# Batched x·yᵀ on one core: 24 unrolled groups rewritten as a loop of 4 iterations over 6 groups, with staggered semaphore resets and the loads of an iteration at its head

## The chip, the cores and the metric

One core of a Trainium2 chip. The metric is the device time of one execution in microseconds (us). Each experiment was timed in rounds with the kernel before on the same chip. A ratio is the mean time of one kernel's fast runs over that of the other's in the same rounds, so it is not quite the ratio of the medians quoted beside it.

Engines: PE is TensorE, DVE is VectorE, ACT is ScalarE, POOL is GpSimd, SP is the sync engine, which issues all transfers here. "L52" is line 52 of the kernel profiled.

## The reference

```python
def setup_inputs():
    batch, n_heads, seq_t, seq_s, channels = 8, 12, 512, 512, 64
    ...  # x, y: (8, 12, 512, 64) float32

def reference(x, y):
    return np.einsum('bhtc,bhsc->bhts', x, y).astype(np.float32)
```

The inputs are 25.2 MB together, the output 100.7 MB. Each byte is moved once.

## The kernel before

The 96 heads are taken in 24 groups of four. A group loads y and x (512 KB each), casts them to bf16 on POOL, transposes them on PE, multiplies on PE, copies the products from PSUM to SBUF on ACT and DVE, and stores 4 MB. Everything is unrolled in Python, so every address is a constant.

```python
    xv = x.rearrange("b h t c -> (b h t c)").rearrange("(g p n) -> g p n", p=P, n=R * C)
    ...  # yv and ov alike
    lpool = ctx.enter_context(tc.tile_pool(name="lpool", bufs=6))
    ...  # bpool 2, tpool 2, opool 4 buffers; PSUM: ptpsum 2, pmpsum 3

    def load(g):
        xs = lpool.tile([P, R * C], fp32)
        ys = lpool.tile([P, R * C], fp32)
        nc.sync.dma_start(ys, yv[g])
        nc.sync.dma_start(xs, xv[g])
        loaded[g] = (xs, ys)

    for g in range(6):
        load(g)

    def prepare(g, made):
        xs, ys = loaded.pop(g)
        ...  # cast y and x to bf16 on POOL
        if g + 6 < NG:
            load(g + 6)                      # prefetch, as soon as the buffers are cast
        yield
        ...  # transposes on PE, copies to SBUF on DVE and ACT, in three steps

    for g in range(NG):
        ...
        steps = prepare(g + 1, made) if g + 1 < NG else iter(())
        ot = opool.tile([P, R, S], fp32)
        edge = g == 0 or g == NG - 1
        for k in range(K):
            ...  # 8 matmuls into pm; copy pm to ot on ACT (even k) or DVE (odd k)
            if edge and k % 2 == 1:
                nc.sync.dma_start(ov[g][:, a:b], ...)          # four pieces of 1 MB
        if not edge:
            nc.sync.dma_start(ov[g], ot.rearrange("p r s -> p (r s)"))   # 4 MB
```

Of the kernel before, what the change touches and what calls it, by code (L numbers as in the profile page):

```python
# [1 line left out]

# [5 lines left out]


@with_exitstack  # L10
def kernel(
    ctx: ExitStack,
    tc: tile.TileContext,
    x: bass.AP,
    y: bass.AP,
    out: bass.AP,
):



    nc = tc.nc
    B, H, T, C = x.shape
    _, _, S, _ = y.shape
    P = 128
    G = 4
    Q = P // G
    R = T // Q
    NG = B * H // G
    K = R // 2
    fp32 = mybir.dt.float32  # L30
    bf16 = mybir.dt.bfloat16
    assert C * 2 == P and S == T and R == 16

    xv = x.rearrange("b h t c -> (b h t c)").rearrange("(g p n) -> g p n", p=P, n=R * C)
    yv = y.rearrange("b h t c -> (b h t c)").rearrange("(g p n) -> g p n", p=P, n=R * C)
    ov = out.rearrange("b h t s -> (b h t s)").rearrange("(g p n) -> g p n", p=P, n=R * S)

    const = ctx.enter_context(tc.tile_pool(name="const", bufs=1))
    lpool = ctx.enter_context(tc.tile_pool(name="lpool", bufs=6))
    bpool = ctx.enter_context(tc.tile_pool(name="bpool", bufs=2))  # L40
    tpool = ctx.enter_context(tc.tile_pool(name="tpool", bufs=2))
    opool = ctx.enter_context(tc.tile_pool(name="opool", bufs=4))
    ptpool = ctx.enter_context(tc.tile_pool(name="ptpsum", bufs=2, space=bass.MemoryType.PSUM))
    pmpool = ctx.enter_context(tc.tile_pool(name="pmpsum", bufs=3, space=bass.MemoryType.PSUM))

    loaded = {}

    def load(g):
        xs = lpool.tile([P, R * C], fp32)
        ys = lpool.tile([P, R * C], fp32)  # L50
        nc.sync.dma_start(ys, yv[g])
        nc.sync.dma_start(xs, xv[g])  # L52
        loaded[g] = (xs, ys)

    for g in range(6):
        load(g)

    ident = const.tile([P, P], bf16)
    make_identity(nc, ident)

    def prepare(g, made):

        xs, ys = loaded.pop(g)
        yb = bpool.tile([P, R, 2, C], bf16)
        nc.gpsimd.tensor_copy(  # L65
            yb, ys.rearrange("p (r c) -> p r c", c=C).unsqueeze(2).to_broadcast([P, R, 2, C])
        )
        xb = bpool.tile([P, R * C], bf16)
        nc.gpsimd.tensor_copy(xb, xs)  # L69
        if g + 6 < NG:  # L70
            load(g + 6)
        yield
        yT = tpool.tile([P, G * Q, R], bf16)
        xT = tpool.tile([P, K, P], bf16)
        for half in range(2):
            pt = ptpool.tile([P, K, P], bf16)
            for k in range(K):
                nc.tensor.transpose(  # L78
                    pt[:, k, :], yb[:, half * K + k].rearrange("p a c -> p (a c)"), ident
                )  # L80
            dst = yT[:, :, half * K:(half + 1) * K]
            src = pt.rearrange("p k n -> p n k")
            if half == 0:
                nc.vector.tensor_copy(dst, src)  # L84
            else:
                nc.scalar.activation(dst, src, mybir.ActivationFunctionType.Copy)  # L86
            yield
        pt = ptpool.tile([P, K, P], bf16)
        for k in range(K):
            nc.tensor.transpose(pt[:, k, :], xb[:, k * P:(k + 1) * P], ident)  # L90
        nc.vector.tensor_copy(xT, pt)  # L91
        made[g] = (xT, yT.rearrange("p n k -> p (n k)"))
        yield

    made = {}
    for _ in prepare(0, made):
        pass
    for g in range(NG):
        xT, yT = made.pop(g)
        steps = prepare(g + 1, made) if g + 1 < NG else iter(())  # L100
        ot = opool.tile([P, R, S], fp32)
        edge = g == 0 or g == NG - 1
        for k in range(K):
            if k % 2 == 0:
                next(steps, None)
            pm = pmpool.tile([P, 2, S], fp32)
            for h in range(G):
                for par in range(2):
                    nc.tensor.matmul(  # L109
                        pm[h * Q:(h + 1) * Q, par, :],  # L110
                        xT[par * C:(par + 1) * C, k, h * Q:(h + 1) * Q],
                        yT[par * C:(par + 1) * C, h * S:(h + 1) * S],
                        start=True, stop=True,
                    )
            if k % 2 == 0:
                nc.scalar.activation(ot[:, 2 * k:2 * k + 2, :], pm, mybir.ActivationFunctionType.Copy)  # L116
            else:
                nc.vector.tensor_copy(ot[:, 2 * k:2 * k + 2, :], pm)  # L118
            if edge and k % 2 == 1:
                a, b = (2 * k - 2) * S, (2 * k + 2) * S  # L120
                nc.sync.dma_start(ov[g][:, a:b], ot.rearrange("p r s -> p (r s)")[:, a:b])
        if not edge:
            nc.sync.dma_start(ov[g], ot.rearrange("p r s -> p (r s)"))  # L123


# [1 line left out]
_INS = ['x', 'y']  # L127
_OUTS = [((8, 12, 512, 512), 'float32')]


# [23 lines left out]
```

## Time and profile before

| | before |
|---|---|
| time | 309.24 us, median of 2 runs (309.17 to 309.3) |
| DMA | 126 MB, mean 410 GB/s, q1 takes 96.7% of 16 engines' span |
| PE, DVE, ACT busy | 51%, 51%, 39% |
| instruction fetches (q8) | 16 |
| issue of a 4 MB store to its landing | 36.6 us |

From the page: the span, the busy share of the DMA engines in 40 slices (tenths, 9 is 90% or more) with the rate in GB/s, the queues, the chain of waits that ended last, and the issues with their median time to landing.

```profile
span 307.5 us, 4865 instructions
...
DMA  7999999999999999999999999999999999999970
GB/s 288 417 376 425 449 405 462 412 427 435 415 436 429 404 450 420 432 436 409 448 426 404 457 420 413 451 412 443 428 431 431 437 431 420 439 432 426 410 302 21
...
q1 hardware_dynamic: 11232, 125.83, 96.7%
q8 instruction: 16, 0.26, 0.3%
...
DMA 72%; DVE 11%; PE 2%; issue 1%; ACT 1%; POOL 1%; SPq 0%; DVEq 0%; ACTq 0%
...
out_dram<-ot SPq DMA_DIRECT2D x22, 4096.0 KB, 36.6
ys<-in_y_dram SPq DMA_DIRECT2D x24, 512.0 KB, 35.7
```

The DMA row is full from the second slice to the last but two: the kernel is bound by transfers.

The waits of SP in the same kernel (in order: who waited, for what, us in total, how often, longest) show what it is held by. L123 is the store, L51 and L52 are the loads:

```profile
SPq L52 <- DMA out_dram<-ot: 130.1, 15, 9.9
SPq L123 <- DVE ot L118: 76.5, 21, 12.3
```

In this trace a store waits for the copy that makes its data (now and then for a load). Loads wait for a landed store because at most eight transfers are out at once: the trace never has more than eight issued and not landed (the compiled program has eight lanes on which landings are reported; the ninth load of the trace is issued at 4.54 us, after the first has landed at 4.08).

### The profile page before, as it was taken

The numbers are of one execution on the slowest core, as the hardware profiler recorded it, in microseconds if no ns is written. First come the engines' busy times: TensorE is split into PE (matmuls) and PEld (weight loads), VectorE is DVE, ScalarE is ACT, GpSimd is POOL, SyncE is SP. The second block draws the span as 40 slices with busy tenths as digits, with TensorE's granted clock in tenths as the row PEclk, the third lists the DMA queues.
The fourth block names the chain that finished last, engine by engine and source line by source line (L and its number), as shares of the span: only waits on it lengthen the run. The fifth ranks groups of instructions, "written<-read, shape, count | busy, mean of one in ns | idle before, by whom it ended". The sixth has DMA issues, their size and how long they took to land.

```text
span 307.5 us, 4865 instructions
## 1 busy us (share of the span) xinstructions
PE 158.3 (51%) x2112; PEld 81.2 (26%) x2112; DVE 157.3 (51%) x144; ACT 119.1 (39%) x121; POOL 70.6 (23%) x54
## 2 busy tenths in 40 slices
PE   2877775483564735648447474383754854320000
PEld 2443342341322313224133241231413412000000
DVE  0599997275373643736537356373563775340000
ACT  1587856144162341623506336053261564330000
POOL 5863354132122221222212312132121000000000
PEclk9999998556655667575575755757555575555555
DMA  7999999999999999999999999999999999999970
GB/s 288 417 376 425 449 405 462 412 427 435 415 436 429 404 450 420 432 436 409 448 426 404 457 420 413 451 412 443 428 431 431 437 431 420 439 432 426 410 302 21
DMA packets 11253, 126.14 MB, mean 410 GB/s; under 512 B 1248, under 2 KB 1248, under 8 KB 7392
## 3 DMA queue, kind: packets, MB, share of 16 engines
q1 hardware_dynamic: 11232, 125.83, 96.7%
q8 instruction: 16, 0.26, 0.3%
q14 instruction: 5, 0.04, 0.0%
HBM read 25.17 MB, written 100.66 MB: 409 GB/s over the span
## 4 chain that ended last, share of the span: by engine, by line
DMA 72%; DVE 11%; PE 2%; issue 1%; ACT 1%; POOL 1%; SPq 0%; DVEq 0%; ACTq 0%
DMA out_dram<-ot 71%; DVE ot L118 8%; DVE yT L84 2%; PE pm L109 1%; DMA ys<-in_y_dram 1%; ACT ot L116 1%; DVE xT L91 1%; PE pt L78 1%; POOL yb L65 1%; PE pt L90 0%; ACT yT L86 0%; SPq L123 0%; DVEq L118 0%; ACTq L116 0%
## 5 line engine op out<-in xcount | busy, mean ns | idle before, releaser
L118 DVE COPY ot<-pm 128x1024 f32<-128x1024 f32 x96 | 114.8, 1221 | 91.0 <-DMA out_dram<-ot 77.2
L116 ACT ACTIVATE ot<-pm 128x1024 f32<-128x1024 f32 x96 | 96.0, 1023 | 143.9 <-DMA out_dram<-ot 121.2
L109 PE MATMUL pm<-yT,xT 64*32 64x512 bf16 x1536 | 98.0, 555 | 100.6 <-ACT ot L116 84.0
L109 PEld LDWEIGHTS <-xT 64*32 64x32 bf16 x1536 | 30.0, 96 | 156.2 <-issue 142.9
L65 POOL CAST yb<-ys 128x2048 bf16<-128x2048 f32 x24 | 45.5, 1896 | 96.9 <-DMA ys<-in_y_dram 79.6
L78 PE MATMUL pt<-ident,yb 128*128 128x128 bf16 x384 | 42.8, 278 | 7.2 <-POOL yb L65 6.1
L69 POOL CAST xb<-xs 128x1024 bf16<-128x1024 f32 x24 | 25.0, 1042 | 65.1 <-PE pt L90 65.1
L78 PEld LDWEIGHTS <-yb 128*128 128x128 bf16 x384 | 35.5, 131 | 15.5 <-issue 7.8
L84 DVE COPY yT<-pt 128x1024 bf16<-128x1024 bf16 x24 | 29.2, 1215 | 7.2 <-PE pt L78 7.2
L90 PE MATMUL pt<-ident,xb 128*128 128x128 bf16 x192 | 26.4, 284 | 5.6 <-ACT yT L86 4.9
L86 ACT ACTIVATE yT<-pt 128x1024 bf16<-128x1024 bf16 x24 | 24.5, 1019 | 8.6 <-PE pt L78 8.6
L91 DVE COPY xT<-pt 128x1024 bf16<-128x1024 bf16 x24 | 16.6, 690 | 17.5 <-PE pt L90 17.5
L90 PEld LDWEIGHTS <-xb 128*128 128x128 bf16 x192 | 16.9, 127 | 18.1 <-issue 18.1
L86 ACT ACT_TABLE_LOAD x1 | 1.3, 1283 | 0.7 <-PEq L138 0.7
masks.py:199 POOL TENSOR_SCALAR_AFFINE_SELECT ident<-ident 128x128 bf16<-128x128 bf16 x1 | 0.3, 294 | 0.1
masks.py:197 POOL MEMSET ident<- 128x128 bf16 x1 | 0.2, 205 | 0.3 <-POOLq L138 0.3
L138 POOL MEMSET const-float32-0.0<- 128x1 f32 x1 | 0.1, 99 | 0.2 <-issue 0.2
L138 POOL MEMSET const-bfloat16-1.0<- 128x1 bf16 x1 | 0.1, 102 | 0.0
L138 POOL MEMSET const-uint8-127<- 128x1 uint8 x1 | 0.1, 102 | 0.0
L138 POOL MEMSET const-float32-1.0<- 128x1 f32 x1 | 0.1, 99 | 0.0
## 6 DMA issues: line engine op xcount, KB each, us to landing
out_dram<-ot SPq DMA_DIRECT2D x22, 4096.0 KB, 36.6
ys<-in_y_dram SPq DMA_DIRECT2D x24, 512.0 KB, 35.7
xs<-in_x_dram SPq DMA_DIRECT2D x24, 512.0 KB, 27.3
out_dram<-ot SPq DMA_DIRECT2D x8, 1024.0 KB, 23.6
```

The costliest lines, as they stand in the source:

```text
L65: nc.gpsimd.tensor_copy(yb, ys.rearrange("p (r c) -> p r c", c=C).unsqueeze(2).to_broadcast([P, R, 2, C]))
L69: nc.gpsimd.tensor_copy(xb, xs)
L78: nc.tensor.transpose(pt[:, k, :], yb[:, half * K + k].rearrange("p a c -> p (a c)"), ident)
L84: nc.vector.tensor_copy(dst, src)
L86: nc.scalar.activation(dst, src, mybir.ActivationFunctionType.Copy)
L90: nc.tensor.transpose(pt[:, k, :], xb[:, k * P:(k + 1) * P], ident)
L91: nc.vector.tensor_copy(xT, pt)
L109: nc.tensor.matmul(pm[h * Q:(h + 1) * Q, par, :], xT[par * C:(par + 1) * C, k, h * Q:(h + 1) * Q], yT[par * C:(par + 1) * C, h * S:(h + 1) ...
L116: nc.scalar.activation(ot[:, 2 * k:2 * k + 2, :], pm, mybir.ActivationFunctionType.Copy)
L118: nc.vector.tensor_copy(ot[:, 2 * k:2 * k + 2, :], pm)
L138: nc = _bacc.Bacc("TRN2", target_bir_lowering=False, num_devices=1)
```

## The change

The intent is less code: one body of six groups, which the engines run four times, instead of 24 copies. With the staggered mode, the body is cut into four stages and semaphores are reset stage by stage instead of behind a barrier. The loads of an iteration come at its head. The addresses are now a register (the loop's variable) plus a constant. The core of the diff:

```diff
+    BODY = 6
-    ov = out.rearrange("b h t s -> (b h t s)").rearrange("(g p n) -> g p n", p=P, n=R * S)
+    ov = out.rearrange("b h t s -> (b h t s)").rearrange("(r n) -> r n", n=R * S)
     ... (xv, yv alike)
-        nc.sync.dma_start(ys, yv[g])
-        nc.sync.dma_start(xs, xv[g])
+        nc.sync.dma_start(ys, yv[bass.ds(g, P)])
+        nc.sync.dma_start(xs, xv[bass.ds(g, P)])
     ...
-        if g + 6 < NG:
-            load(g + 6)
     ...
-    for g in range(NG):
+    with tc.For_i(0, NG * P, BODY * P, iteration_sync="staggered") as g0:
+        loaded = [load(g0 + i * P) for i in range(BODY)]
     ... (prepare the first group, then)
+        for i in range(BODY):
     ...
-        edge = g == 0 or g == NG - 1
+            edge = i == 0
     ...
-        if not edge:
-            nc.sync.dma_start(ov[g], ot.rearrange("p r s -> p (r s)"))
+            if not edge:
+                nc.sync.dma_start(ov[bass.ds(g0 + i * P, P)], ot.rearrange("p r s -> p (r s)"))
```

More of the change, by code (lines that the diff above doesn't have):

```diff
@@ L32 @@
     assert C * 2 == P and S == T and R == 16
-    xv = x.rearrange("b h t c -> (b h t c)").rearrange("(g p n) -> g p n", p=P, n=R * C)
-    yv = y.rearrange("b h t c -> (b h t c)").rearrange("(g p n) -> g p n", p=P, n=R * C)
-    ov = out.rearrange("b h t s -> (b h t s)").rearrange("(g p n) -> g p n", p=P, n=R * S)
+    xv = x.rearrange("b h t c -> (b h t c)").rearrange("(r n) -> r n", n=R * C)
+    yv = y.rearrange("b h t c -> (b h t c)").rearrange("(r n) -> r n", n=R * C)
+    ov = out.rearrange("b h t s -> (b h t s)").rearrange("(r n) -> r n", n=R * S)
     const = ctx.enter_context(tc.tile_pool(name="const", bufs=1))
@@ L44 @@
     pmpool = ctx.enter_context(tc.tile_pool(name="pmpsum", bufs=3, space=bass.MemoryType.PSUM))
-    loaded = {}
+    ident = const.tile([P, P], bf16)
+    make_identity(nc, ident)
     def load(g):
@@ L50, in load, with prepare @@
         ys = lpool.tile([P, R * C], fp32)
-        nc.sync.dma_start(ys, yv[g])
-        nc.sync.dma_start(xs, xv[g])
-        loaded[g] = (xs, ys)
-    for g in range(6):
-        load(g)
-    ident = const.tile([P, P], bf16)
-    make_identity(nc, ident)
-    def prepare(g, made):
-        xs, ys = loaded.pop(g)
+        nc.sync.dma_start(ys, yv[bass.ds(g, P)])
+        nc.sync.dma_start(xs, xv[bass.ds(g, P)])
+        return xs, ys
+    def prepare(xs, ys, made):
         yb = bpool.tile([P, R, 2, C], bf16)
@@ L91, in prepare @@
         nc.vector.tensor_copy(xT, pt)
-        made[g] = (xT, yT.rearrange("p n k -> p (n k)"))
+        made.append((xT, yT.rearrange("p n k -> p (n k)")))
         yield
-    made = {}
-    for _ in prepare(0, made):
-        pass
-    for g in range(NG):
-        xT, yT = made.pop(g)
-        steps = prepare(g + 1, made) if g + 1 < NG else iter(())
-        ot = opool.tile([P, R, S], fp32)
-        edge = g == 0 or g == NG - 1
-        for k in range(K):
-            if k % 2 == 0:
-                next(steps, None)
-            pm = pmpool.tile([P, 2, S], fp32)
-            for h in range(G):
-                for par in range(2):
-                    nc.tensor.matmul(
-                        pm[h * Q:(h + 1) * Q, par, :],
-                        xT[par * C:(par + 1) * C, k, h * Q:(h + 1) * Q],
-                        yT[par * C:(par + 1) * C, h * S:(h + 1) * S],
-                        start=True, stop=True,
-                    )
-            if k % 2 == 0:
-                nc.scalar.activation(ot[:, 2 * k:2 * k + 2, :], pm, mybir.ActivationFunctionType.Copy)
-            else:
-                nc.vector.tensor_copy(ot[:, 2 * k:2 * k + 2, :], pm)
-            if edge and k % 2 == 1:
-                a, b = (2 * k - 2) * S, (2 * k + 2) * S
-                nc.sync.dma_start(ov[g][:, a:b], ot.rearrange("p r s -> p (r s)")[:, a:b])
-        if not edge:
-            nc.sync.dma_start(ov[g], ot.rearrange("p r s -> p (r s)"))
@@ new lines @@
+    with tc.For_i(0, NG * P, BODY * P, iteration_sync="staggered") as g0:
+        loaded = [load(g0 + i * P) for i in range(BODY)]
+        made = []
+        for _ in prepare(*loaded[0], made):
+            pass
+        for i in range(BODY):
+            xT, yT = made[i]
+            steps = prepare(*loaded[i + 1], made) if i + 1 < BODY else iter(())
+            ot = opool.tile([P, R, S], fp32)
+            edge = i == 0
+            for k in range(K):
+                if k % 2 == 0:
+                    next(steps, None)
+                pm = pmpool.tile([P, 2, S], fp32)
+                for h in range(G):
+                    for par in range(2):
+                        nc.tensor.matmul(
+                            pm[h * Q:(h + 1) * Q, par, :],
+                            xT[par * C:(par + 1) * C, k, h * Q:(h + 1) * Q],
+                            yT[par * C:(par + 1) * C, h * S:(h + 1) * S],
+                            start=True, stop=True,
+                        )
+                if k % 2 == 0:
+                    nc.scalar.activation(ot[:, 2 * k:2 * k + 2, :], pm, mybir.ActivationFunctionType.Copy)
+                else:
+                    nc.vector.tensor_copy(ot[:, 2 * k:2 * k + 2, :], pm)
+                if edge and k % 2 == 1:
+                    a, b = (2 * k - 2) * S, (2 * k + 2) * S
+                    nc.sync.dma_start(
+                        ov[bass.ds(g0 + i * P, P), a:b],
+                        ot.rearrange("p r s -> p (r s)")[:, a:b],
+                    )
+            if not edge:
+                nc.sync.dma_start(ov[bass.ds(g0 + i * P, P)], ot.rearrange("p r s -> p (r s)"))
```

## The prediction

> **What bounds it now.** The DMA engines. The page gives DMA 97% of 16 engines' span, 126 MB at 410 GB/s; PE and DVE are busy 51%. The chain of waits is 71% store landings. Compute has slack: unstalled (timeline, 18 to 43 us) a group takes 6.25 us; at a granted clock of 0.5 about 7.5 us (an estimate: eight matmuls took 0.6 us, a transpose 0.11). In the steady part a group's traffic takes 12.65 us: two loads of 1.24 us and a store of 10.15 us, by the steps between landings.
>
> One DMA engine is the limit: from 300 to 306 us the windows read a DMA share of 0.06, one engine of 16. The landing records show its lag behind the next engine growing by about 0.4 us per group until 277 us, then standing at 6.5 us. The 16 instruction fetches of 16 KB (queue q8, about 0.95 us each) run from 18 to 258 us, so I take the lag to be these: at this engine's 26 GB/s each costs 0.63 us, 10 us in all. That all ride on one engine is inferred.
>
> **What the change does.**
> - Traffic and arithmetic stay: 12.65 x 6 = 76 us of DMA per iteration.
> - Prefetch across groups goes: 12 loads at an iteration's head (14.9 us), queued behind the last iteration's stores, then six stores. At the start of before, the first store was issued 10.8 us after ys had landed; with 1.3 us for that landing, 12.1 us, inside the 14.9 us of loads. Group 1's store follows 10 us later (24.9 against 14.9 us), as group 0's pieces take 10.1 us. So the queue hardly empties: 0 to 1 us in all.
> - Stage waits: I expect each quarter of the body to wait until the stores of the quarter two before have landed. Compute per iteration is some 6 x 7 + 12 us plus four refills of 2 to 3 us, about 65 us of 76. The next loads should be issued with two groups of stores still queued, some 14 us ahead. Hidden.
> - Code: PE's body is about 1056 instructions plus waits[...]. [...] No trace here shows a loop yet. If PE keeps its body, fetches fall to about 5 and time falls by up to 6.4 us (the next engine's lag).
> - Start and end: register set-up and the loop's exit, +1 us (a guess).
>
> **Sum.** 309.2 + 3 (fetches) + 1 (ends) + 0 to 1 (bubbles) = **313.5 us**, 8 in 10 within 308 to 321. Chances: faster by over 2% 0.04, within 2% 0.66, slower 0.30.
>
> **What would show it.** DMA share at 0.9 or more in nearly all slices; at most shallow dips at about 79, 155 and 231 us. q8 packets 20 to 24. ACT, DVE and PE idle some 14 us at each boundary, ended by the ys DMA. Chain still DMA above 65%. A single DMA engine at the end.
>
> **What would make it wrong.** Stage waits that hold SP or an engine until the store queue is empty: the DMA row would show holes below 0.7, and the time would be 325 or more. Slow DMA issue from register addresses (over 1.2 us each against 0.33 to 0.45 now) would starve the head. Fewer fetches: 303 to 308.

The 3 us for fetches was the author's estimate: 4 to 8 fetches more than the 16 of before, at 0.63 us each (16 KB at the 26 GB/s that the windows of before read from 300 to 306 us). Of these, the number of fetches was not shown; the 20 to 24 packets further down rest on it too. Estimates, without a trace, are also the "about 5" fetches and the four refills of 2 to 3 us (before has no stages to show one).

## The result, and the profile after

The kernel after takes 375.5 us (374.78 and 376.22) against 309.24: a ratio of 1.214, with 95% interval 1.204 to 1.224. The prediction was 313.5 us, 308 to 321.

The lines of the page after that answer to those shown of before:

```profile
span 373.0 us, 5474 instructions
...
DMA  6956877999986688797987759887999766998877
GB/s 201 409 203 286 365 341 337 394 394 394 343 332 231 275 358 373 337 390 341 450 324 294 281 225 394 383 348 337 394 394 368 278 268 267 394 394 373 358 337 337
...
q1 hardware_dynamic: 12096, 125.83, 82.1%
q8 instruction: 3, 0.05, 0.0%
...
DMA 66%; issue 17%; SPq 4%; DVE 1%; PE 1%; ACT 0%; ACTq 0%
...
out_dram<-ot SPq DMA_DIRECT2D x20, 4096.0 KB, 11.1
out_dram<-ot SPq DMA_DIRECT2D x16, 1024.0 KB, 4.0
ys<-in_y_dram SPq DMA_DIRECT2D x24, 512.0 KB, 11.3
```

The DMA row has holes nearly everywhere, not only at the three boundaries. The chain is still mostly DMA, so that share tells nothing here. What tells is the time to landing: 11.1 us in place of 36.6. Each 4 MB store now meets an empty queue. The waits of SP name the reason (L121 is the whole store, L116 the 1 MB piece):

```profile
SPq L121 <- DMA out_dram<-ot: 171.9, 16, 11.0
SPq L116 <- DMA out_dram<-ot: 40.2, 12, 5.5
```

SP no longer waits for the copy but for the landing of another store: 28 times, 212 us. In the chain of waits, in order of time (start, us, what), the second iteration reads:

```profile
112.93 5.96 DMA out_dram<-ot
...
119.06 3.99 DMA out_dram<-ot
...
123.07 3.83 DMA out_dram<-ot
...
131.67 11.37 DMA out_dram<-ot
...
143.19 11.13 DMA out_dram<-ot
...
154.45 11.09 DMA out_dram<-ot
...
165.67 11.09 DMA out_dram<-ot
```

Each store is issued only when the one before it has landed. The compiled program shows the wait: the waits of SP's stores, in order of issue, by the lanes on which transfers report their landing (a number and the stage; the first piece and the last two stores of the body are left out):

```
31 L116 DMACopy out_0_dram<-ot_153 128x2048 [waits DMAHW1_I-81_stg1, ...]
33 L116 DMACopy out_0_dram<-ot_153 128x2048 [waits DMAHW2_I-81_stg1]
35 L116 DMACopy out_0_dram<-ot_153 128x2048 [waits DMAHW0_I-81_stg2]
37 L121 DMACopy out_0_dram<-ot_274 128x8192 [waits DMAHW1_I-81_stg2]
39 L121 DMACopy out_0_dram<-ot_392 128x8192 [waits DMAHW0_49, ...]
41 L121 DMACopy out_0_dram<-ot_510 128x8192 [waits DMAHW1_49, ...]
```

Each waits for the lane of the store just before it. In the packet records of the trace, no DMA engine at all moves anything for 54.6 us in all, in 37 gaps, most of 1.2 to 1.5 us. Before had none once its first load was under way. An iteration takes 92.2 us (first load issued at 85.98, 178.19 and 270.40 us) instead of some 76.

My first theory: with register addresses, the framework's dependency tracking cannot tell the stores' targets in the output apart, takes them to overlap, and orders them by waits. Rivals: the staggered stages hold SP and the engines; or the lost prefetch (loads at the head) starves the queue.

### The profile page after: what moved, and what is told of

It is laid out like the page before. It is cut to its first block, busy times and chain, and to the rows that moved or that the text cites. A ratio compares the mean times of both kernels' runs of the same rounds, so it can differ in the third digit from the quotient of the medians.

```text
span 373.0 us, 5474 instructions
## 1 busy us (share of the span) xinstructions
PE 130.1 (35%) x2112; PEld 65.6 (18%) x2112; DVE 152.9 (41%) x144; ACT 124.8 (33%) x124; POOL 69.6 (19%) x54
## 4 chain that ended last, share of the span: by engine, by line
DMA 66%; issue 17%; SPq 4%; DVE 1%; PE 1%; ACT 0%; ACTq 0%
DMA out_dram<-ot 54%; DMA ys<-in_y_dram 12%; SPq L54 2%; SPq L53 1%; DVE ot L113 1%; SPq L88 1%; PE pm L104 1%; SPq L121 1%; SPq L116 1%; ACT ot L111 0%; SPq L147 0%; ACTq L111 0%
## 5 line engine op out<-in xcount | busy, mean ns | idle before, releaser
L111 ACT ACTIVATE ot<-pm 128x1024 f32<-128x1024 f32 x96 | 97.4, 1023 | 62.2 <-PE pm L104 38.7
L104 PE MATMUL pm<-yT,xT 64*32 64x512 bf16 x1536 | 80.0, 433 | 51.9 <-ACT ot L111 26.3
L71 PE MATMUL pt<-ident,yb 128*128 128x128 bf16 x384 | 41.3, 248 | 146.1 <-POOL yb L60 143.8
L71 PEld LDWEIGHTS <-yb 128*128 128x128 bf16 x384 | 28.7, 112 | 166.8 <-POOL yb L60 146.2
L104 PEld LDWEIGHTS <-xT 64*32 64x32 bf16 x1536 | 24.1, 91 | 85.5 <-issue 62.3
L83 PE MATMUL pt<-ident,xb 128*128 128x128 bf16 x192 | 21.7, 246 | 2.8 <-DVE yT L77 2.8
L83 PEld LDWEIGHTS <-xb 128*128 128x128 bf16 x192 | 14.4, 110 | 12.4 <-issue 12.3
## 6 DMA issues: line engine op xcount, KB each, us to landing
out_dram<-ot SPq DMA_DIRECT2D x20, 4096.0 KB, 11.1
ys<-in_y_dram SPq DMA_DIRECT2D x24, 512.0 KB, 11.3
xs<-in_x_dram SPq DMA_DIRECT2D x24, 512.0 KB, 11.9
```

The source lines that it names most:

```text
L71: nc.tensor.transpose(pt[:, k, :], yb[:, half * K + k].rearrange("p a c -> p (a c)"), ident)
L83: nc.tensor.transpose(pt[:, k, :], xb[:, k * P:(k + 1) * P], ident)
L104: nc.tensor.matmul(pm[h * Q:(h + 1) * Q, par, :], xT[par * C:(par + 1) * C, k, h * Q:(h + 1) * Q], yT[par * C:(par + 1) * C, h * S:(h + 1) ...
L111: nc.scalar.activation(ot[:, 2 * k:2 * k + 2, :], pm, mybir.ActivationFunctionType.Copy)
```

## The experiments

| kernel | median us | ratio to before (95%) |
|---|---|---|
| after | 375.5 | 1.214 (1.204 to 1.224) |
| free_stores | 326.55 | 1.055 (1.053 to 1.057) |
| free_stores_bounds | 321.19 | 1.038 (1.036 to 1.039) |
| bounds_only | 387.58 | 1.252 (1.250 to 1.254) |
| unrolled_ordered | 342.8 | 1.108 (1.104 to 1.111) |
| unrolled_head | 309.45 | 1.000 (0.998 to 1.002) |
| free_stores_late | 314.36 | 1.016 (1.013 to 1.019) |
| free_stores_barrier | 324.34 | 1.049 (1.046 to 1.052) |
| free_stores_prefetch | 314.62 | 1.016 (1.013 to 1.018) |
| unrolled_head_ordered | 373.81 | 1.208 (1.206 to 1.210) |
| free_stores_short | 326.68 | 1.056 (1.054 to 1.057) |
| free_stores_even | 315.62 | 1.019 (1.018 to 1.021) |

Every one gave correct results.

### free_stores: the loop without the order of stores

```diff
+from concourse.bass_types import dram_disjoint_views
-    ov = out.rearrange("b h t s -> (b h t s)").rearrange("(r n) -> r n", n=R * S)
+    ov = dram_disjoint_views(out.rearrange(...).rearrange("(r n) -> r n", n=R * S), BODY - 1 + K // 2)
...
-                        ov[bass.ds(g0 + i * P, P), a:b],
+                        ov[BODY - 1 + k // 2][bass.ds(g0 + i * P, P), a:b],
...
-                nc.sync.dma_start(ov[bass.ds(g0 + i * P, P)], ...)
+                nc.sync.dma_start(ov[i - 1][bass.ds(g0 + i * P, P)], ...)
```

Nine names for the same output, which the dependency tracker takes as disjoint on the author's word. A gentler try was only built: a separate constant index for the group (the register picks the iteration, the constant the group) left every wait in place.

> The loop with the output named through nine views that the dependency tracker takes as disjoint, so no store waits for the one before it; stage boundaries as they fall. Theory 1 (stores in a loop are addressed by a register, so each was ordered behind the landing of the one before): the steps between stores fall from 11.25 us to about 10.1 us (4.5 us an iteration) and most of the extra 8.6 us of the four 1 MB pieces goes; what stays is the hole where the twelfth load and the first pieces wait for a stage boundary (about 3 us) and a like one at the fourth piece. 326 us, 318 to 334. Theory 2 (the staggered stages are the cost, the store order only follows from them): 365 to 375 us. Theory 3 (the cost is the lost prefetch, loads at the head of an iteration): 365 to 375 us.

Measured: 326.55 us. In SP's part of the compiled program the waits between stores are gone, and little else changed but the stage in which some of them fall. So the order of the stores is worth 49 of the 66 us. The gaps with no transfer at all fall from 54.6 to 11.8 us, and the page shows the DMA row full but for one dip per iteration:

```profile
DMA  5969999999986999999996899999999499999994
GB/s 194 416 230 423 459 415 436 444 432 415 368 357 216 431 448 444 399 444 448 357 414 273 294 452 411 448 448 420 424 372 416 189 367 464 424 415 450 424 424 198
...
out_dram<-ot SPq DMA_DIRECT2D x20, 4096.0 KB, 24.4
```

The dip, in windows of the same kernel (stretch, its length, busy time of each engine with instructions, granted clock, DMA share, GB/s):

```profile
94.00:98.00 4.00, 3.73 (x54) 1.97 (x51) 4.00 (x4) 3.34 (x4) 1.91 (x2) 0.70 0.62 248
98.00:100.50 2.50, 2.08 (x35) 0.66 (x35) 2.50 (x4) 1.50 (x3) 1.25 (x2) 1.00 0.00 0
100.50:104.00 3.50, 3.09 (x61) 1.78 (x61) 3.50 (x4) 3.34 (x4) 1.61 (x1) 1.00 0.96 302
```

For 2.5 us nothing moves while PE and DVE work. In SP's program a stage boundary falls between the eleventh and the twelfth load, and SP may not cross it before the other engines have reached their own (stage boundaries are explained under bounds_only). The pieces of group 0 that are ready wait behind it: the twelfth load is issued at 99.70 us and the first piece at 100.30 us.

### unrolled_head and unrolled_head_ordered: the same without a loop

unrolled_head writes the body out four times, with constant addresses (group 0 of each six is stored in four pieces here too):

```diff
-    with tc.For_i(0, NG * P, BODY * P, iteration_sync="staggered") as g0:
+    for g0 in range(0, NG * P, BODY * P):
-        nc.sync.dma_start(ys, yv[bass.ds(g, P)])
+        nc.sync.dma_start(ys, yv[g:g + P])
     ... (all addresses alike)
```

> The body of the loop written out four times without a loop: same instructions, loads of six groups at the head of each run of six, fixed addresses, so neither ordered stores nor stages. It measures the lost prefetch by itself. By the sum of the prediction (first store 12.1 us after the head's loads begin, loads take 14.9 us) it costs nothing: 309 to 313 us. If loads at the head are what keeps the freed loop at 321 to 326: 318 us or more.

Measured: 309.45 us, a ratio of 1.000, and its DMA row is full:

```profile
DMA  7999999999999999999999999999999999999991
...
out_dram<-ot SPq DMA_DIRECT2D x20, 4096.0 KB, 23.4
```

Loads at the head of six groups cost nothing: the third theory falls, and the prediction's sum for the head was right. The view of the output is the same as in the kernel after, and with constant addresses no store waits for the one before it.

unrolled_head_ordered adds one thing to it, the wait of each store for the one before, and pins the loads to their place (in unrolled_ordered, below, nothing is pinned and loads lie between the waiting stores). The pins change no order: by its trace, unrolled_head also issues its twelve loads, then four pieces and five stores, then the next twelve.

```diff
+    stores = []
+    def store(dst, src):
+        now = nc.sync.dma_start(dst, src)
+        if stores:
+            tc.add_manual_dep(now.ins, stores[-1].ins.name,
+                mybir.DependencyInfo(mybir.DependencyClass.Sync, mybir.DependencyReason.DATA))
+        stores.append(now)
     ... (store(...) in place of nc.sync.dma_start for the two stores; each load gets a
         DependencyClass.NoSync edge on stores[-1], which keeps its order and waits for nothing)
```

> unrolled_head with each store made to wait for the landing of the one before, the loads kept at their place: the sync engine's order of the loop as changed, without the loop. It closes a table of two by two: unrolled or loop, stores free or ordered (309.4, 326.5, 375.5 known). From the steps measured in the loop as changed: four pieces at 3.95 us instead of 2.43 and four whole stores at 11.25 instead of 9.7 in each run of six (the fifth has loads queued behind it), so 6.1 + 6.2 = 12.3 us, 49 us in all, and up to 1 us for each code fetch that meets an empty queue: 309 + 49 + 0 to 10 = 358 to 368 us. If the order of stores costs as much only in a loop: under 345 us.

(The 1 us for a fetch is an estimate; the packet of one takes 0.88 to 1.07 us in the trace of before.)

Measured: 373.81 us, 64 us above unrolled_head and above the expected range of 358 to 368. Its profile has the pattern of the kernel after, without a loop, a stage or a register address:

```profile
SPq L53 <- DMA out_dram<-ot: 265.4, 32, 13.0
...
out_dram<-ot SPq DMA_DIRECT2D x20, 4096.0 KB, 11.1
```

| | stores free | stores ordered |
|---|---|---|
| unrolled, loads at head | 309.45 | 373.81 |
| loop, staggered stages | 326.55 | 375.5 |

The order of stores alone is enough for nearly the whole loss. The two costs do not add: the loop costs 17 us with free stores and some 2 us with ordered ones. Two things differ on the ordered row. Unrolled code still fetches its instructions (16 fetches), and some meet a store that is alone (next experiment): the first whole store of a six takes 13.0 to 13.1 us with a fetch in its time, in the last three sixes, against 11.4 us in the kernel after, which fetches 3 times in all. And a stage's wait may lie partly inside a wait that the order imposes anyway; no run shows that by itself. How much each contributes was not separated.

### unrolled_ordered: the kernel before, stores ordered

The same `store` function in the kernel before; nothing pinned, so the loads of the prefetch come to lie between the stores.

> The kernel before, unrolled, with each store made to wait for the landing of the one before it, nothing else. Theory 1 in its fine form (ordering costs only where no load is queued behind a store to fill the gap): about 0 in the first 200 us, where each store is followed by two loads; then some 1.1 us for each of the last five whole stores and 1.5 us for each of the eight pieces: 309 + 6 + 10 = 322 us at most, 314 to 324. If ordering alone cost 1.1 us on each store whatever is queued: 309 + 22 + 12 = 343. Theories 2 and 3: 309 us.

Measured: 342.8 us, 34 above before. My "fine form" was wrong (314 to 324), and the plain count, 1.1 us a store and 1.5 us a piece whatever is queued, came out at 343. That agreement is partly luck. In the middle, where each store has two loads queued behind it, a group takes 13.07 us (97.52 to 175.94 us over six) against 12.65 before, so the loads do hide most of it. But after 202 us, 14 of the 30 stores still have to go with no loads left. They read, in the chain of waits:

```profile
202.07 13.19 DMA out_dram<-ot
215.40 12.96 DMA out_dram<-ot
228.45 11.76 DMA out_dram<-ot
240.33 11.32 DMA out_dram<-ot
251.79 13.02 DMA out_dram<-ot
264.89 13.28 DMA out_dram<-ot
278.30 11.18 DMA out_dram<-ot
```

The first of these still shares its time with the last two loads (landed at 205.6 us). In the rest, 16 KB instruction fetches begin at 224.2, 239.6, 259.4 and 276.2 us. The four stores in whose time one begins take 11.8 to 13.3 us; the two without take 11.2 and 11.3. The three whole stores that follow have no such fetch: two take 11.1 us, and the one at 289.61 us takes 11.9, with an 8 KB fetch (queue q14) in its time. So a fetch is visible where a store is alone and its landing is waited for. It holds up one engine: in the landing records of the three slowest (13.0 to 13.3 us), fifteen of the sixteen engines land within 0.4 us, and the last one 1.6 to 2.1 us later.

### bounds_only: stores ordered, stage boundaries moved

```diff
+            if i in (0, 1, 3):
+                tc.stage_boundary()
```

> The loop as changed, stores still ordered, only the stage boundaries set after groups 0, 1 and 3. Theory 1: the hole ahead of the first piece (2.9 us) and the stretch of the pieces beyond 16 us (2.7 us) go, 5 us an iteration: 353 us, 348 to 360; stores still 11.2 us apart. Theory 2: it falls under 330 us.

Measured: 387.58 us, slower than the kernel after by 12 instead of faster by 22. The timeline shows why (start, us, engine, line, what, [idle before it]):

```profile
113.42 16.24 SPq L116 DMA_DIRECT2D out_dram<-ot  x4
...
117.19 1.21 DVE L113 COPY ot<-pm 128x1024 f32<-128x1024 f32 x1
130.09 1.05 PE L104 MATMUL pm<-yT,xT 64*32 64x512 bf16 x16 [13.62 <-issue]
```

All four pieces of group 0 now belong to the first stage. SP issues the last one, held back by the order, at 129.3 us; only then does it reach the next stage, and PE, done since 116.5 us, may not enter it before SP does. So a stage boundary makes an engine wait for the slowest one's program order, SP's issues included: here PE sat idle for 13.62 us and POOL for 19.87. I had treated it as a wait for landings of two stages back only.

### free_stores_bounds and free_stores_late: where the boundaries fall, stores free

free_stores_bounds is free_stores with the two lines of bounds_only added (boundaries after groups 0, 1 and 3). free_stores_late puts them after group 1, in the middle of group 3 and after group 4:

```diff
+                if i == 3 and k == 3:
+                    tc.stage_boundary()
...
+            if i in (1, 4):
+                tc.stage_boundary()
```

> As free_stores, and the stage boundaries set by hand after groups 0, 1 and 3, so that all twelve loads and all four pieces of group 0 lie in the first stage. If store order and the place of the boundaries are all of the cost, 76 to 77 us an iteration is left: 308 to 313 us. If the staggered waits or the loads at the head cost more than that, 318 us or more. If the fetches of PE's code were what made one DMA engine late in the kernel before, the lag of the last engine at the end is under 2 us here (three fetches) and the time can fall to 304.

> The freed loop with the stage boundaries after group 1, in the middle of group 3 and after group 4, so that every boundary is crossed with a whole store or more queued. If the holes of free_stores_bounds came from crossing a boundary with a short queue (there 3 us an iteration ahead of group 1's store), they go, and an iteration takes 73.5 us (12 loads of 1.28 us and six stores of 9.68 us as measured in the freed loop's undisturbed stretches) to 76 us: 299 to 310 us in all. If each crossing costs something of its own whatever is queued: 318 us or more, as free_stores_bounds.

Measured: 321.19 us and 314.36 us. Both missed their ranges (308 to 313, and 299 to 310). The hole of the first sits ahead of group 1's store:

```profile
104.00:108.00 4.00, 4.00 (x56) 1.94 (x48) 3.30 (x3) 2.96 (x3) 0.00 (x0) 0.50 0.93 391
108.00:111.00 3.00, 0.60 (x16) 0.00 (x0) 2.01 (x3) 1.02 (x1) 0.00 (x0) 0.93 0.04 16
111.00:115.00 4.00, 2.61 (x41) 1.13 (x42) 2.14 (x2) 1.17 (x2) 3.94 (x3) 0.60 1.23 524
```

The engines finished group 0 and could not begin group 1 until SP had issued its last piece, so the transfer of group 1's store began some 3 us after group 0's had drained. With the boundary after group 1, that hole shrinks to about 1.1 us (103.5 to 105.5 us in free_stores_late). So of the 17 us that the loop costs with free stores, the place of the boundaries accounts for 12. What free_stores_late keeps over unrolled_head is 5 us. 1.4 us of that are a later start (first load at 2.11 instead of 0.74 us). The rest was not taken apart; the packet records show dips of 0.3 to 1.1 us at the boundaries.

### free_stores_barrier: the plain barrier between iterations

`iteration_sync="staggered"` taken out of free_stores.

> The freed loop with the plain barrier between iterations instead of the staggered stages. No stage in the body, but the DMA queue empties three times. Between the last byte of a store and the first of the next load I expect 3 to 4 us of hole (landing, barrier, issue), and none elsewhere: 314 us, 308 to 322, so faster than free_stores with its staggered stages as they fall (326). If the staggered stages do their work, the barrier costs more: 335 us or more.

Measured: 324.34 us, so like the staggered loop as its boundaries fell (326.55), but above the expected 314 and its range. The hole without any transfer at each boundary is 3.0 to 3.1 us, as expected. What I left out is what lies around it: the engines of the DMA run dry one after another, and the first loads after the barrier run at 163 to 380 GB/s for some 5 us. By the packet records, one boundary (77 to 89 us) loses about 6 us of full rate in all.

### free_stores_prefetch: the loads of the next iteration issued early

The input buffers are kept outside the loop, loaded ahead of it and refilled for the next iteration when a group has been cast; three iterations in the loop, the last written out behind it.

```diff
+    for i in range(BODY):
+        load(i, i * P)
...
         nc.gpsimd.tensor_copy(xb, xs)
+        if g_next is not None:
+            load(i, g_next + i * P)
...
+    with tc.For_i(0, (NG - BODY) * P, BODY * P, iteration_sync="staggered") as g0:
+        body(g0, False)
+    body((NG - BODY) * P, True)
```

> The freed loop with the loads of the next iteration issued as soon as a group's buffers have been cast (six groups of input kept in buffers made outside the loop, loaded ahead of it), three iterations in the loop and the last written out behind it; stage boundaries after groups 1, 2 and 4. No head of loads, and little code fetched. If the remaining cost is at the head and at boundaries with a short queue, 24 groups at 12.3 us and 5 us of ends: 300 us, 297 to 308. If the staggered crossing or the loop's entry and exit cost more, 312 us or more.

Measured: 314.62 us, above the range. Inside the loop the rate holds. The loss sits at the loop's exit, where the program waits at a barrier for all engines and transfers before the last six groups may start:

```profile
240.00:244.00 4.00, 2.35 (x21) 2.19 (x22) 1.23 (x1) 1.39 (x2) 4.00 (x4) 0.50 0.51 217
244.00:248.00 4.00, 3.22 (x46) 1.45 (x43) 1.40 (x2) 1.16 (x2) 3.76 (x3) 0.50 0.08 33
248.00:252.00 4.00, 3.79 (x62) 1.98 (x61) 4.00 (x5) 2.98 (x3) 2.34 (x2) 0.71 0.68 270
```

That is 12 us at a mean DMA share of 0.42, some 7 us lost.

### free_stores_short and free_stores_even: two tries to beat the unrolled kernel

From free_stores_late: groups 1 and 3 also stored in four pieces, third boundary moved to the middle of group 4.

```diff
-            edge = i == 0
+            edge = i in (0, 1, 3)
...
+                if i in (3, 4) and k == 3:
+                    tc.stage_boundary()
...
+            if i == 1:
+                tc.stage_boundary()
```

> free_stores_late with groups 1 and 3 also stored in four pieces (so group 1's store starts before group 0's has drained, where 1.1 us of hole were left) and the third stage boundary moved from behind group 4 to the middle of it (so that the next loads are issued with a whole store more in the queue; they came about 3 us ahead of its end, and about 1.6 us of transfer were lost there). About 3 us in each of four iterations should come back: 314 - 10 = 304 us, 301 to 310, so perhaps the first loop that is faster than the unrolled kernel. If a loop of staggered stages has a cost that no placing removes: 313 to 316 us.

Measured: 326.68 us, 12 us slower than free_stores_late and far above the range. PE sits idle ahead of group 4's second half until the pieces of the stage two before have landed:

```profile
129.66 1.22 DVE L114 COPY ot<-pm 128x1024 f32<-128x1024 f32 x1
136.96 1.01 PE L72 MATMUL pt<-ident,yb 128*128 128x128 bf16 x8 [8.71 <-issue]
```

By storing group 3 in pieces I had put its first half into the second stage, and the fourth stage opens only when that has landed. free_stores_even stores group 3 whole again (`edge = i in (0, 1)`).

> free_stores_short with group 3 stored whole again. There its first half fell into the second stage, so the fourth stage could open only when that half had landed, with 2 MB left in the queue (5 us) against some 6 us to group 4's store: a hole of 4 us in each iteration (138 to 143 us). With group 3 whole, the second stage ends with group 2's store, the fourth opens with all of group 3 still queued, and the hole should go: under 314 us, 304 expected, 301 to 310. If pieces of group 1 or the moved boundary were what cost 12 us: 320 us or more.

Measured: 315.62 us. The 11 us came back, so that explanation holds. But the time stayed above the range, and the hoped-for 304 did not come: the dips moved to other boundaries (by the packet records a busy share of 0.43 in 114 to 116 us and 0.81 in 134 to 136). No loop tried here is faster than the unrolled kernel before.

## Why the prediction was wrong

**The step that failed** is "Prefetch across groups goes: 12 loads at an iteration's head (14.9 us), queued behind the last iteration's stores, then six stores. [...] So the queue hardly empties: 0 to 1 us in all." The head was right (unrolled_head: 309.45 us). The words "then six stores" were not right: they took the six stores as issued when their data is ready, as before. With register addresses, each waited for the landing of the one before it. That is an extra wait which the diff does not spell out, and the compiled program does. In its place the runs showed 49 us between free_stores and after, and 64 us between the two unrolled kernels.

What one ordered store costs: alone it lands 11.1 us after its issue. Queued behind another it adds 9.7 us (the last three landings of free_stores: 304.11, 313.79, 323.47 us). A 1 MB piece takes 3.8 to 4.0 us instead of 2.4. So a link of an ordered chain costs 1.4 us more than a store in a full queue, and 1.4 to 1.6 us for a piece; the gaps with no transfer between stores are mostly 1.2 to 1.5 us. No run here takes that apart. The cost is paid once per link of a chain; in a deep queue it does not show in the steps between landings (9.7 us).

**Stage waits** ("Hidden") were wrong in size: 17 us for the loop with the boundaries as they fell, 5 us with them placed well (1.4 us of each is the later start). They were mis-stated too. A boundary waits not only for the stores of two stages back, but for every engine, SP among them, to have come to the end of its own previous stage (bounds_only: PE idle 13.6 us for SP).

**Instruction fetches** (+3 us) went the other way: I expected 20 to 24 in place of 16, which no trace had shown; there were 3 (at 18, 26 and 35 us), all in the first iteration. What that is worth in time was not measured. In three jumps back, PE's body of 1073 rows was not fetched again. The prediction named the alternative ("If PE keeps its body") and gave it too little weight.

**The lag of one DMA engine** as the work of fetches is not settled. free_stores_bounds was to test it: with 3 fetches its lag at the end is 0.5 us, under the 2 us named beforehand. But its queue runs empty once an iteration, as the queue of the kernel after does at every store (a lag of at most 0.3 us in its last eight landings), and there the lag did not add up from store to store. In favour: the stores that meet a fetch are slower in unrolled_ordered (11.8 to 13.3 us against 11.2 and 11.3). Against: unrolled_head has the same 16 fetches and a lag of 3.3 us instead of 6.4 at the same time, and free_stores_late has 3 fetches and a lag of 3.7 us.

**Start and end** (+1 us) was about right: the first load is issued 1.7 us later.

**The warnings** under "What would make it wrong": the first named the outcome, 325 us or more with holes in the DMA row, but put it down to stage waits. Free of its store order, the loop took 326.55 us: that is the warned-of cost. The other 49 us come from a wait that I had not considered. The second, slow issue from register addresses, did not come true: the issue of a load took at most 1.12 us in the kernel after, and up to 1.27 us in unrolled_head_ordered, whose addresses are constants.

## What to carry to other kernels

When constant addresses become register addresses, ask whether the framework can still tell two accesses to the same tensor apart. If it cannot, it adds waits that no line of the diff shows (here 28, 212 us in all), so read the wait list of the issuing engine, and give it disjoint views where you can vouch for them. In a profile, the time from issue to landing tells a deep queue (36.6 us here) from a chain of one (11.1 us), while "the chain is mostly DMA" is true of both. In a loop cut into stages, put every boundary where enough transfer is queued to cover the engines' refill (321.19 us became 314.36), and ask which landings of earlier stages it waits for (free_stores_short lost 12 us to them).
